# How the last squares of a norm are summed: VectorE for all eight feature tiles, and one product per token block in place of two

## The chip, the core and the metric

The kernel runs on one core of one Trainium2 chip. The core has a matrix engine (TensorE, in the profile PE, with its weight loads as PEld), a vector engine (VectorE, DVE), a scalar engine (ScalarE, ACT), a general one (GpSimd, POOL) and one that issues most transfers (SyncE, SP). Each takes its instructions in the order of its own queue and waits on semaphores for the others. The metric is the device time of one execution in microseconds (us). A change of under 0.5% is about what a measurement of this kernel cannot tell from none.

## The reference, cut to what matters

The program is one step of a two-layer model over 640 tokens of 1024 features: 512 latent tokens and 128 context tokens. Layer 0 mixes tokens by attention, layer 1 by a gated linear recurrence, and a gated feed-forward block (FFN) follows each. Ahead of each of these four sub-layers stands a normalisation, and a last one stands at the end:

```python
def _rms_norm(x, g):
    xf = x.astype(jnp.float32)
    y = xf * lax.rsqrt(jnp.mean(xf * xf, axis=-1, keepdims=True) + RMS_EPS)
    return (y * g.astype(jnp.float32)).astype(x.dtype)

def _modulate(x, g, shift, scale):
    return _rms_norm(x, g) * (1 + scale[:, None, :]) + shift[:, None, :]
```

Scale, shift and a gate for the residual come from a conditioning vector by a product with `w_mod`; latent and context tokens have their own. What the change touches is the sum of the squares over the features of a token.

## The kernel before, in words

**Layout.** Features lie on the 128 partitions, in eight tiles (`KT = 8`), tokens along the free axis. `x[:, k]` is feature tile k of the residual stream. Tokens are worked on in chunks: `CH` is 0 to 320 and 320 to 640, `CHL` is 0 to 384 and 384 to 640. A weight tile is split into a high and a low part (`unit` L163, `two` L185, `split` L1068: ScalarE casts, VectorE subtracts, L182 or L1070), and `chunk` (L209) makes a product of three matmuls for each feature tile: high by high (L217), high by low (L218), low by high (L219). Its result lies in one of a few accumulators: three with the name `mm`, and in some phases two or three named `mx`. A chunk can start only when the accumulator that it takes has been read.

**A norm.** A projection produces the new x tile by tile. For each tile and chunk `residual` (L437) adds the gated product to x on VectorE (L440) and calls `square` (L370). This squares the tile on ScalarE (L376 for tile 0, straight into the sum `ssq`; L379 into a buffer `sq`, of which there are two) and adds tiles 1 to 6 to `ssq` on VectorE (L381). The last tile, 7, isn't added: its squares are kept in `lastq`. Then `moment` (L387) sums over the partitions on TensorE: for each block of 128 tokens a single-precision product of `ssq` with a column of ones (L393), and a second one of tile 7's squares into the same place (L396). The profile records each such product as two instructions. In a chunk of 320 the third block overlaps the second. VectorE makes the variance from it (`var`, L398), GpSimd raises it to the power -1/2 (`rs`, L400), VectorE spreads that over a diagonal (`dg`, L402), and `spread` (L405) multiplies the diagonal by ones on TensorE (L410), so that each partition has the factor of each token.

**The five norms.** The first, at the start, sums all eight tiles in `ssq` by its own code (`load_x` in `start`, L316) and uses one product for each block, since `lastq` is still empty. The other four use `square`:

1. *Norm 1*, in `project` (L444) after the attention projection, ahead of the first FFN. The FFN's first matmuls use x before its normalisation; the factor is applied when their results are read (`rt`, L709 and L717). Meanwhile VectorE is filled with modulation products (L247), whose weights GpSimd loads (L243) into two buffers.
2. *Norm 2*, in `project_closing` (L458), which ends the first layer. Its chunks are those of `CHL`. The second chunk of the last six feature tiles is left to the end, and between its steps the first chunk is normalised: `normed` (L467) calls `modulate` (L413), that is L415 on VectorE, L416 on ScalarE, L417 on VectorE. Tiles 6 and 7 of this wait, by an order written by hand, behind `self.sq`, the newest addition to `ssq`. The recurrent layer's first chunk (`x0[0]` in `run`, L1183) then begins, and from feature tile 3 on it stands behind `self.at`, the last product of the sum; the next one stands behind the spread (`self.rr`), and the weight split of its unit behind `self.sq`.
3. *Norm 3*, in `project_halves` (L779) after the recurrence, ahead of the second FFN, with the chunks of `CH`. Its factor is copied by ScalarE (L799), and `first_half` (L752) normalises the first chunk (L746, L747) while the second is projected. The FFN's first products (`plain`, L891) are held behind `self.at` and `self.rr` too (`held`, L832).
4. *The final norm*, in `project_last` (L498).

**What sets the order.** Within each engine a scheduler places the instructions by its own estimate of times; orders written by hand (`issue_after`) bind it. An engine never passes a waiting instruction.

The `tail` list that is set at the start isn't used.

## Time and profile before

| | us |
|---|---|
| median of the three runs | 1538.77 |
| the three runs | 1538.27, 1538.77, 1543.96 |
| the profiled execution | 1538.44 |
| its span, first to last instruction | 1536.3 |

Of the span TensorE is busy for 97%, VectorE for 69%, ScalarE for 45%, GpSimd for 16%. The mean granted clock of TensorE was 0.989 of full speed.

The rows of the timeline that are shown below begin with the start in us from the span's start and the time in us that the row lasts, then the engine, the source line, the operation, the tile that it writes, an arrow, and the tiles that it reads, with their shapes; `x2` means two instructions merged. In brackets stand the idle time of the engine just before and what ended it. Matmuls overlap in these rows, so the pace of TensorE is read from starts, not from durations. In the list of waits the three numbers are us in total, times, and the longest. In the table of windows the columns are the window, its length, the busy us (and instructions) of PE, PEld, DVE, ACT and POOL, the granted clock, the share of the transfer engines, and GB/s.

The three norms of the change lie at about 382 to 401 us (norm 1), 839 to 870 us (norm 2) and 1058 to 1090 us (norm 3); the final one begins near 1515 us.

### The profile page before, as it was taken

Reading aid. Unit: us, or ns where it says so; the run is one execution under the profiler, and the core shown is the slowest. Engines: PE = TensorE matmul, PEld = TensorE weight load, DVE = VectorE, ACT = ScalarE, POOL = GpSimd, SP = SyncE. Lnnn points to the kernel's source line nnn. Section 1 sums busy time; section 2 is a strip of 40 time slices with the busy share of each in tenths; the row PEclk is TensorE's granted clock in tenths of the full one; section 3 lists DMA queues with packets and bytes.
Section 4 is the critical chain, followed back from the end, with each engine's and each line's share of the span. In section 5 each row is a group of like instructions: output and inputs, shape, how many; then the busy total and the mean of one; then the engine's idle time right before and its main releaser. Section 6 shows DMA issues by size and latency. Waiting matters only on the chain. (4 is left out here: it accounts for less than half of the span.)

```text
span 1536.3 us, 25993 instructions
## 1 busy us (share of the span) xinstructions
PE 1483.2 (97%) x10309; PEld 1437.0 (94%) x10309; DVE 1060.9 (69%) x2000; ACT 695.3 (45%) x1266; POOL 253.2 (16%) x270
## 2 busy tenths in 40 slices
PE   5999999989999999999999999989999999999997
PEld 3899999889999999999999988889999999999996
DVE  5668788869899987434443869874965656556556
ACT  5576667755333123312331478853544342424242
POOL 2101122100111110000000113220222322222210
PEclk9999999999999999999999999999999999999998
DMA  9545656545566664222223533334242231323211
GB/s 378 154 115 162 182 157 184 145 136 187 178 194 191 194 215 124 72 83 76 71 61 106 153 119 110 107 130 142 85 135 71 81 102 64 98 68 97 70 56 69
DMA packets 73098, 196.65 MB, mean 128 GB/s; under 512 B 8048, under 2 KB 25616, under 8 KB 72848
## 3 DMA queue, kind: packets, MB, share of 16 engines
q1 hardware_dynamic: 58832, 144.48, 29.6%
q0 software_dynamic: 13856, 50.35, 10.5%
q8 instruction: 81, 1.33, 0.4%
q14 instruction: 41, 0.34, 0.1%
q10 hardware_dynamic: 288, 0.16, 0.0%
HBM read 179.48 MB, written 8.92 MB: 123 GB/s over the span
## 5 line engine op out<-in xcount | busy, mean ns | idle before, releaser
L217 PE MATMUL mm<-big,whi 128*128 128x320 f32 (+3 forms) x1290 | 400.1, 313 | 9.0 <-ACT big L1069 7.3
L218 PE MATMUL mm<-big,whi 128*128 128x320 f32 (+3 forms) x1290 | 402.9, 313 | 2.9 <-DVE big L1070 2.2
L219 PE MATMUL mm<-big,wlo 128*128 128x320 f32 (+3 forms) x1290 | 401.9, 312 | 1.9 <-DVE wlo L182 1.6
L217 PEld LDWEIGHTS mm<-big,whi 128*128 128x128 f32 x1290 | 243.6, 190 | 13.5 <-ACT big L1069 8.2
L218 PEld LDWEIGHTS mm<-big,whi 128*128 128x128 f32 x1290 | 244.9, 190 | 6.6 <-DVE big L1070 4.3
L219 PEld LDWEIGHTS mm<-big,wlo 128*128 128x128 f32 x1290 | 244.4, 190 | 3.7 <-DVE wlo L182 2.1
L247 DVE SCALAR_TENSOR_TENSOR mprod<-mraw,csb 128x1024 f32<-128x1024 f32 x160 | 195.5, 1222 | 8.7 <-DMA mraw<-in_wm 8.4
L440 DVE SCALAR_TENSOR_TENSOR x<-mm,G,x 128x128 f32<-128x128 f32 (+3 forms) x211 | 85.5, 435 | 92.1 <-PE mm L219 91.8
L182 DVE TENSOR_TENSOR wlo<-raw,whi 128x1024 fp32r<-128x1024 f32 (+1 forms) x90 | 109.8, 1220 | 38.0 <-ACT whi L180 23.1
L180 ACT CAST whi<-raw 128x1024 fp32r<-128x1024 f32 (+1 forms) x74 | 76.8, 1037 | 121.0 <-PE mm L218 81.8
L217 PE MATMUL mm<-big,whx 128*128 128x320 f32 (+3 forms) x363 | 113.3, 312 | 0.0
L219 PE MATMUL mm<-big,wlx 128*128 128x320 f32 (+3 forms) x363 | 113.0, 311 | 0.0
L218 PE MATMUL mm<-big,whx 128*128 128x320 f32 (+3 forms) x363 | 112.7, 311 | 0.0
L243 POOL DMA_DIRECT2D mraw<-in_wm x80 | 43.3, 542 | 381.3 <-DVE mprod L247 259.1
L217 PE MATMUL mx<-big,whi 128*128 128x320 f32 (+3 forms) x278 | 86.6, 311 | 0.0
L219 PE MATMUL mx<-big,wlo 128*128 128x320 f32 (+3 forms) x278 | 86.3, 310 | 0.0
L218 PE MATMUL mx<-big,whi 128*128 128x320 f32 (+3 forms) x278 | 86.3, 310 | 0.0
L180 ACT CAST whx<-raw 128x1024 fp32r<-128x1024 f32 (+1 forms) x40 | 41.0, 1027 | 90.6 <-PE mm L218 55.1
L217 PE MATMUL mx<-big,whx 128*128 128x320 f32 (+3 forms) x245 | 75.8, 309 | 0.0
L219 PE MATMUL mx<-big,wlx 128*128 128x320 f32 (+3 forms) x245 | 75.6, 309 | 0.0
L218 PE MATMUL mx<-big,whx 128*128 128x320 f32 (+3 forms) x245 | 75.4, 308 | 0.0
L1069 ACT CAST whi<-raw 128x1024 fp32r<-128x1024 f32 (+1 forms) x41 | 41.3, 1008 | 72.8 <-PE mm L218 45.1
(295 smaller groups left out, 3602.9 us busy)
## 6 DMA issues: line engine op xcount, KB each, us to landing
raw<-in_gu SPq DMA_DIRECT2D x88, 512.0 KB, 3.6
mraw<-in_wm POOLq DMA_DIRECT2D x80, 512.0 KB, 4.1
raw<-in_dn SPq DMA_DIRECT2D x24, 512.0 KB, 3.7
raw<-in_wqk SPq DMA_DIRECT2D x16, 512.0 KB, 4.3
raw<-in_wi SPq DMA_DIRECT2D x16, 512.0 KB, 3.6
whi<-in_wi POOLq DMA_DIRECT2D x16, 512.0 KB, 4.4
raw<-in_dn SPq DMA_DIRECT2D x16, 448.0 KB, 3.4
sw<-in_wm SPq DMA_DIRECT2D x10, 512.0 KB, 10.1
```

Source lines behind the costliest of these rows:

```text
L180: nc.scalar.copy(hi, raw)
L182: nc.vector.tensor_tensor(lo, raw, hi.bitcast(F32), ALU.subtract)
L217: nc.tensor.matmul(ps, hi[:, k], xhi[:, k, s], start=(k == 0), stop=False)
L218: nc.tensor.matmul(ps, hi[:, k], xlo[:, k, s], start=False, stop=False)
L219: nc.tensor.matmul(ps, lo[:, k], xhi[:, k, s], start=False, stop=(k == nk - 1))
L243: nc.gpsimd.dma_start(w, self.i["wm"][l * 6 + j - 2, f])
L247: nc.vector.scalar_tensor_tensor(prod, w, 1.0, self.csb[:, s], ALU.mult, ALU.mult, accum_out=out[:, s, f:f + 1])
L440: self.nc.vector.scalar_tensor_tensor(xs, ps[:, a - t0:b - t0], G[:, s, f:f + 1], xs, ALU.mult, ALU.add)
L1069: self.nc.scalar.copy(hi, v)
```

## The change

In norms 1, 2 and 3 tile 7's squares are now added to `ssq` by VectorE like those of the others, and each block has one product. A flag `apart`, set in `project_last`, keeps the final norm as it was. `self.sq` is thereby the addition of tile 7 in the inner norms, and `self.at` the one product of the last block.

```diff
-        self.anchor, self.pbufs, self.lastq, self.tail = None, {}, {}, []
+        self.anchor, self.pbufs, self.lastq, self.apart = None, {}, {}, False
...
         q = self.t([P, 384], F32, "sq", 2, self.sb)[:, :t1 - t0]
         nc.scalar.activation(q, self.x[:, k, s], AF.Square)
-        if k < KT - 1:
+        if k == KT - 1 and self.apart:
+            self.lastq[t0] = q
+        else:
             self.sq = nc.vector.tensor_tensor(self.ssq[:, s], self.ssq[:, s], q, ALU.add).ins
-        self.lastq[t0] = q
...
         for j, b in enumerate(bl):
-            nc.tensor.matmul(ps[:, j:j + 1], self.ssq[:, b:b + P], self.ones[:, 0:1], start=True, stop=not self.lastq)
-            if not self.lastq:
+            self.at = nc.tensor.matmul(ps[:, j:j + 1], self.ssq[:, b:b + P], self.ones[:, 0:1], start=True, stop=not self.apart).ins
+            if not self.apart:
                 continue
             self.at = nc.tensor.matmul(ps[:, j:j + 1], self.lastq[t0][:, b - t0:b - t0 + P], self.ones[:, 0:1], start=False, stop=True).ins
...
-        first = None
+        first, self.apart = None, True
```

## The prediction, made before the changed kernel ran

> **What bounds the kernel now.** I read the page's busy line first, then what TensorE (PE) waited for, then the timeline of each engine around the three inner norms.

> ```profile
> PE 1483.2 (97%) x10309; PEld 1437.0 (94%) x10309; DVE 1060.9 (69%) x2000; ACT 695.3 (45%) x1266; POOL 253.2 (16%) x270
> ```

> ```profile
> PE mm L217 <- ACT big L1069: 7.3, 3, 6.2
> ...
> PE mx L410 <- DVE dg L402: 2.6, 2, 1.9
> ...
> PE at L393 <- DVE ssq L381: 2.0, 2, 1.7
> ```

> PE is busy for 97% of the span, and its largest wait on one cause is 7.3 us in all: what leaves PE's queue is a gain, unless a new wait takes it back. The lower two rows (total, times, longest) are waits of norms: the sum product (L393) for the sum of squares, the spread (L410) for the diagonal. The longer of each, 1.7 and 1.9, is in the final norm, which stays as it is.

> **What is removed.** A chunk of 320 or 384 tokens has three blocks of 128 (in 320 the last overlaps), one of 256 has two. The inner norms have 6 + 5 + 6 = 17 blocks, so 17 products of L396 go, each recorded as two instructions.

> ```profile
> 382.44 0.31 PE L217 MATMUL mx<-big,whi 128*128 128x320 f32 x1
> ...
> 384.07 0.31 PE L219 MATMUL mx<-big,wlo 128*128 128x320 f32 x1
> ...
> 385.03 0.36 PE L396 MATMUL at<-ones,sq 128*128 128x1 f32 x2
> 385.25 0.36 PE L393 MATMUL at<-ones,ssq 128*128 128x1 f32 x2
> ```

> Durations overlap, so I go by starts: 385.25 - 385.03 = 0.22 us for a product, (384.07 - 382.44)/11 = 0.148 us for a large matmul of 320 columns. 17 x 0.22 = **3.8 us** is the most that PE saves, or 4.0 with fewer breaks between groups. That is 0.26%, under the 0.5% that a measurement of this kernel can tell from no change.

> **What is added.** Six additions on VectorE (DVE), 0.3 to 0.5 us each, some 2.4 us in all. More matters that each sum now waits for tile 7's addition, and that the scheduler, which knows it, puts the sum products, spreads and their neighbours elsewhere. The built program differs in order only around the three norms and in how the modulation products interleave behind the first. On POOL one modulation load (L243) moves ahead of two powers (L400); on SP two stores of x each pass a neighbour. Those are read much later: I cost the stores at nothing. ScalarE's casts and squares move by a place or two, in its 55% of idle time.

> *Norm 1, after the attention projection.*

> ```profile
> 388.80 0.36 PE L396 MATMUL at<-ones,sq 128*128 128x1 f32 x2
> ...
> 398.40 0.83 PE L410 MATMUL rr<-dg,ones 128*128 128x128 f32 x6
> 398.98 0.39 PE L219 MATMUL mm<-big,wlo 128*128 128x322 f32 x1
> ...
> 401.45 0.31 PE L217 MATMUL mm<-big,whi 128*128 128x320 f32 x1
> ```

> ```profile
> 389.20 0.23 DVE L398 TENSOR_SCALAR var<-at 128x3 f32<-128x3 f32 x2 [3.15 <-PE at L396]
> 389.35 1.21 DVE L247 SCALAR_TENSOR_TENSOR mprod<-mraw,csb 128x1024 f32<-128x1024 f32 x1
> 390.49 0.08 DVE L247 DVE_READ_ACCUMULATOR mprod<-mraw,csb 128x1 f32 x1
> 391.33 0.56 DVE L402 TENSOR_TENSOR dg<-ident,rs 128x384 f32<-128x384 f32 x1 [0.76 <-POOL rs L400]
> 391.81 0.17 DVE L249 TENSOR_TENSOR G<-G,cols 128x16 f32<-128x16 f32 x1
> ```

> In before the two groups of sum products stand apart; now both stand behind 63 large matmuls counted from the one at 382.44: 382.44 + 63 x 0.148 = 391.8, six products end at 393.1, and the variance, 0.4 us after the last product's start as in before, is done at 393.4. DVE then has, in the built order, three modulation products (1.14 each) and two weight splits (as long) ahead of the second diagonal, and two diagonals of 0.48: 393.4 + 5 x 1.14 + 2 x 0.48 = 400.1, so the second spread starts at 400.2. PE is ready for it at 393.1 + 33 x 0.148 + 0.58 (first spread: 398.98 - 398.40) + 5 x 0.148 = 399.3, and waits 0.9 us. The group behind it starts at 400.2 + 0.6 = 400.8 instead of 401.45: **-0.6** of the 1.4 that PE alone would save. The additions lie in DVE's idle 3.15 us. Bounds: -1.4 (no wait); and, for the case that the products just ahead of the second diagonal find their load late, the longest such wait of the stretch behind this norm (total, times, longest):

> ```profile
> DVE mprod L247 <- DMA mraw<-in_wm: 7.9, 10, 1.8
> ```

> With 1.8 us of that and the half clock described below (1.5), -0.6 becomes +2.7.

> *Norm 2, the projection that closes the first layer.* DVE's queue sets the pace here.

> ```profile
> 846.95 0.83 PE L410 MATMUL rr<-dg,ones 128*128 128x128 f32 x6
> ```

> ```profile
> 846.42 0.60 DVE L440 SCALAR_TENSOR_TENSOR x<-mx,G,x 128x128 f32<-128x128 f32 x2
> 846.93 0.60 DVE L440 SCALAR_TENSOR_TENSOR x<-mm,G,x 128x128 f32<-128x128 f32 x2
> 847.56 0.42 DVE L381 TENSOR_TENSOR ssq<-ssq,sq 128x256 f32<-128x256 f32 x1
> 847.90 1.66 DVE L415 SCALAR_TENSOR_TENSOR nv<-x,A,rr 128x384 f32<-128x384 f32 x3
> 849.48 0.42 DVE L381 TENSOR_TENSOR ssq<-ssq,sq 128x256 f32<-128x256 f32 x1
> ...
> 856.46 0.42 DVE L381 TENSOR_TENSOR ssq<-ssq,sq 128x256 f32<-128x256 f32 x1
> 856.79 0.60 DVE L415 SCALAR_TENSOR_TENSOR nv<-x,A,rr 128x384 f32<-128x384 f32 x1
> 857.32 1.22 DVE L182 TENSOR_TENSOR wlo<-raw,whi 128x1024 fp32r<-128x1024 f32 x1
> 858.45 0.60 DVE L415 SCALAR_TENSOR_TENSOR nv<-x,A,rr 128x384 f32<-128x384 f32 x1
> 858.98 0.15 DVE L398 TENSOR_SCALAR var<-at 128x2 f32<-128x2 f32 x1
> ...
> 860.28 0.42 DVE L402 TENSOR_TENSOR dg<-ident,rs 128x256 f32<-128x256 f32 x1
> ```

> ```profile
> 856.92 0.38 PE L393 MATMUL at<-ones,ssq 128*128 128x1 f32 x2 [0.35 <-DVE ssq L381]
> ...
> 860.87 0.66 PE L410 MATMUL rr<-dg,ones 128*128 128x128 f32 x4
> 861.28 0.42 PE L217 MATMUL mm<-big,whi 128*128 128x384 f32 x1
> ```

> The first chunk's spread stands 18 matmuls of 256 columns later (0.148 x 256/320 = 0.12 each), less three products and a break: 846.95 + 2.2 - 0.8 = 848.4. The normalisation (L415) that waits for it moves from 847.90 to 849.35, and from there DVE has no gap before the sum. Up to tile 7's addition its queue holds six L415 (1.58/3 = 0.53 by starts), six L417 taken as long, six updates of x (0.51/2 = 0.26) and two additions (0.33): 8.6 us, so that addition starts at 857.9, against 856.46 for the last one now. PE gets the sum 0.46 us later, at 858.4, but is ready at 856.57 - 0.8 = 855.8: **a wait of 2.6 us where 0.35 stood**. Behind the addition stand a weight split pinned to it (1.13) and two L415, so the variance comes at 860.45, the diagonal 1.3 later as now, the second spread at 862.3, and the recurrent layer's second chunk at 862.7 instead of 861.28. That is **+1.4**, with the two removed products already in it. Queued behind are the L415 and L417 of the second chunk, 1.5 us late too. Bounds: -1.1 (PE alone), +1.4.

> *The half clock.* A wait of that length had a consequence before:

> ```profile
> 1107.60:1109.50 1.90, 0.02 (x1) 0.02 (x1) 1.90 (x4) 0.46 (x1) 0.67 (x1) 1.00 0.23 85
> 1109.50:1113.40 3.90, 3.90 (x16) 3.90 (x17) 3.90 (x11) 0.00 (x0) 0.00 (x0) 0.57 0.27 83
> 1113.40:1117.00 3.60, 3.60 (x27) 3.60 (x26) 3.60 (x7) 3.52 (x7) 2.62 (x2) 0.99 0.60 185
> ```

> After 1.9 us with PE idle (0.02 busy in the first row) the granted clock, third column from the end, was 0.57 over 3.9 us: 16 matmuls where 3.9/0.148 = 26 would fit, so ten are lost, 1.5 us. If 2.6 us do the same, the 15 matmuls of 384 columns between the sum and the spread run at 0.178/0.57 = 0.31 instead of 0.178 us: from 858.9, twelve or thirteen in the 3.9 us and the rest in 0.4 end at 863.2, and the second spread moves from 862.3 to there: **+0.9**, which I take, since the nearest row did it. Bounds: 0 and +1.5 (all of a dip exposed).

> [...]

> *Norm 3, after the recurrent layer.*

> ```profile
> 1080.54 0.68 DVE L440 SCALAR_TENSOR_TENSOR x<-mx,G,x 128x192 f32<-128x192 f32 x2 [1.30 <-PE mx L219]
> ...
> 1081.54 1.68 DVE L381 TENSOR_TENSOR ssq<-ssq,sq 128x320 f32<-128x320 f32 x3
> 1083.13 1.22 DVE L182 TENSOR_TENSOR wlo<-raw,whi 128x1024 fp32r<-128x1024 f32 x1
> ```

> ```profile
> 1088.35 0.91 PE L410 MATMUL mx<-dg,ones 128*128 128x128 f32 x6 [0.79 <-DVE dg L402]
> ```

> The second spread already waits for DVE, whose queue starts with PE's last projection chunk (the release at 1080.54). That chunk comes 0.8 us earlier (three products, one break); one addition makes the queue 0.4 longer, and some of the gaps between its additions close. I take **-0.5**; the rest of PE's saving becomes a longer wait, 1.6 for 0.79. Bounds: -1.4 and +0.4. The dip after 1107.6 I leave as it is.

> **Sum:** -0.6 + 1.4 + 0.9 - 0.5 = +1.2 us. The profiled execution took 1538.44 us around a span of 1536.3 (the median of the three runs is 1538.77): 1538.44 + 1.2 = **1539.6 us**.

> **Rivals.**
> 1. *No half clock at norm 2*: 2.6 us is short enough, or PE waits less because its queue and DVE's are closer than I count. 1538.44 + 0.3 = 1538.7. For it: PE waits for DVE up to the second spread anyway. Against: the 0.57 above. [...]
> 2. *The whole saving arrives*: the additions are in time and the moved spreads cost nothing. 1538.44 - 3.8 = 1534.6, 1534.4 with the breaks. For it: 97% busy, few waits. Against: DVE has no gap between 847.56 and the sum in norm 2.
> 3. *Slower*: PE starves at norm 1 too. The second spread there stands behind five DVE operations of 1.14 us that need loaded weights, and the next chunks have no free accumulator before it. From a wait of some 1.9 us on, the half clock sets in. With the whole queue of 5.7 us and a load 1.8 late exposed: 1538.44 - 1.4 + 5.7 + 1.8 + 1.5 + 2.3 (norm 2) - 0.5 = 1547.8. Against: in before that load lands ahead of its turn, and the moved L243 asks for it earlier still.

> That the products stay is excluded: the built program has none of the 17.

> **How the numbers follow.** Forecast 0.45, rival 1 0.25, rival 2 0.15, rival 3 0.05; the remaining 0.10 is for two starved norms or an exposed dip, about 1541 to 1543. The forecast's own range is 1538.3 to 1541.5. The range that takes in rivals 1 and 2 below and the unknown costs above (1539.6 + 0.6 + 2.7 at norm 1) is 1534.4 to 1542.9. Faster by over 0.5% needs 1530.7, which even 4.0 us cannot give: 0.01. Slower by over 0.5% is 1546.1, rival 3 alone: 0.05. Within: 0.94.

> **What would show it.** (Lines from L381 on stand one or two later in the changed kernel.) The second product left with 10 instructions, all in the final norm; the additions up from 48 to 54. At norm 2 a PE wait of 2 to 3 us for the sum and granted clock near 0.5 in the next 3 us; a second spread some 1.4 us later in step. At norm 1 a PE wait of about 0.9 for the diagonal; at norm 3 one of 1.6. It is wrong if these waits are absent and the time falls by 3 us or more, or if waits appear in the feed-forward blocks between the norms.

## The result, and the profile after

| | median, us | lowest to highest, us | executions |
|---|---|---|---|
| before | 1539.08 | 1535.31 to 1545.32 | 22 |
| after | 1544.35 | 1537.60 to 1549.09 | 22 |

The ratio is 1.0028, 95% interval 1.0017 to 1.0039: 4.3 us slower, between 2.6 and 6.0 (the two medians themselves lie 5.3 apart). That is under 0.5%, as forecast, and yet the interval tells it from none. The changed kernel is slower than the forecast says, and 1544.35 lies above the range. The profiled execution of the changed kernel took 1544.4 us around a span of 1542.5.

The page's busy line shows the work that went and the work that came:

```profile
PE 1484.9 (96%) x10275; PEld 1439.1 (93%) x10275; DVE 1065.1 (69%) x2006; ACT 694.3 (45%) x1266; POOL 254.3 (16%) x270
```

PE has 34 instructions fewer, the 17 second products; VectorE has six more, the additions (L383 now, 54 instead of 48). PE's count fell and its busy time did not: it was 1483.2. The list of waits (total, times, longest) says where to look:

```profile
PE at L394 <- DVE ssq L383: 4.1, 2, 2.4
PE mx L411 <- DVE dg L403: 3.8, 2, 2.0
```

Each of the two rows of norms has grown, from 2.0 and 2.6. The longest wait for a sum is now 2.4 us, and it is no longer in the final norm. The timeline of PE has it in norm 2, a new wait for the second diagonal at norm 1, and a longer one at norm 3 (1.95 us, before 0.79), by which the second row grew:

```profile
402.95 0.91 PE L411 MATMUL rr<-dg,ones 128*128 128x128 f32 x6 [0.58 <-DVE dg L403]
...
832.17 0.34 PE L217 MATMUL mm<-big,whx 128*128 128x384 f32 x1
...
850.61 0.83 PE L411 MATMUL rr<-dg,ones 128*128 128x128 f32 x6
...
860.50 1.01 PE L394 MATMUL at<-ones,ssq 128*128 128x1 f32 x4 [2.40 <-DVE ssq L383]
...
866.32 1.06 PE L411 MATMUL rr<-dg,ones 128*128 128x128 f32 x4
...
876.04 0.38 PE L217 MATMUL mm<-big,whi 128*128 128x256 f32 x1 [0.19 <-ACT xr L1009]
...
1093.77 0.91 PE L411 MATMUL mx<-dg,ones 128*128 128x128 f32 x6 [1.95 <-DVE dg L403]
```

Starts of two profiles can't be compared directly, since one may run late from an earlier point on. So I compare the same large matmul in both, ahead of a norm and behind it. The two rows of L217 above are these in the kernel before:

```profile
830.01 0.34 PE L217 MATMUL mm<-big,whx 128*128 128x384 f32 x1
...
870.36 0.38 PE L217 MATMUL mm<-big,whi 128*128 128x256 f32 x1 [0.37 <-ACT xr L1008]
```

The changed kernel is 832.17 - 830.01 = 2.16 us late ahead of norm 2 and 876.04 - 870.36 = 5.68 behind it: norm 2 costs **+3.52 us**. "In step" below means that the lag ahead of the norm is taken off. Counted in the same way norm 1 gives **-0.61** and norm 3 **-0.05**, together +2.86. Which matmul is taken moves such a step by up to 0.05.

The table of windows, in stretches of 3.41 us, has the rest (window, its length, PE busy, PEld, DVE, ACT, POOL, granted clock, transfer share, GB/s):

```profile
857.09:860.50 3.41, 1.01 (x6) 0.70 (x4) 3.41 (x10) 1.61 (x4) 0.00 (x0) 1.00 0.39 136
860.50:863.91 3.41, 3.41 (x12) 3.41 (x13) 3.32 (x6) 1.14 (x2) 1.06 (x1) 0.50 0.33 77
863.91:867.32 3.41, 3.41 (x14) 3.41 (x13) 1.59 (x3) 0.00 (x0) 0.29 (x7) 0.50 0.34 93
867.32:870.73 3.41, 3.41 (x21) 3.41 (x20) 3.32 (x13) 1.94 (x7) 0.00 (x0) 1.00 0.37 143
```

In the first row PE is busy for 1.01 us; in the next two it has half clock, 6.8 us in all; in the fourth the clock is whole. All 15 matmuls between the sum and the second spread run at half clock (0.32 us from start to start, against 0.17 ahead of the wait), one reason why the page's busy time of PE did not fall. VectorE, busy throughout in the first row, is busy for 1.59 us in the third: now it waits for PE, 1.84 us for the second spread.

The profiled execution is also 2.8 us late before any changed instruction. Of this 2.05 us arise between 290 and 320 us, with half clock in the attention, where this execution has it (two stretches from 300.72 on, the first is shown) and the profiled one of before has not:

```profile
297.30:300.71 3.41, 1.79 (x12) 1.16 (x10) 3.41 (x6) 3.36 (x7) 3.25 (x4) 1.00 0.42 106
300.72:304.13 3.41, 3.06 (x10) 2.66 (x11) 3.41 (x6) 3.41 (x10) 0.43 (x1) 0.50 0.00 0
```

### The profile page after: what moved, and what is told of

Same layout as the page of the kernel before. It is cut to its first block, busy times and chain, and to the rows that moved or that the text cites. A ratio compares the mean times of both kernels' runs of the same rounds, so it can differ in the third digit from the quotient of the medians.

```text
span 1542.5 us, 25932 instructions
## 1 busy us (share of the span) xinstructions
PE 1484.9 (96%) x10275; PEld 1439.1 (93%) x10275; DVE 1065.1 (69%) x2006; ACT 694.3 (45%) x1266; POOL 254.3 (16%) x270
## 5 line engine op out<-in xcount | busy, mean ns | idle before, releaser
L217 PE MATMUL mm<-big,whi 128*128 128x320 f32 (+3 forms) x1290 | 402.4, 315 | 8.9 <-ACT big L1070 7.3
L219 PE MATMUL mm<-big,wlo 128*128 128x320 f32 (+3 forms) x1290 | 404.2, 314 | 1.6 <-DVE wlo L182 1.6
L217 PEld LDWEIGHTS mm<-big,whi 128*128 128x128 f32 x1290 | 245.6, 191 | 13.3 <-ACT big L1070 8.2
L219 PEld LDWEIGHTS mm<-big,wlo 128*128 128x128 f32 x1290 | 246.4, 191 | 3.1 <-DVE wlo L182 2.1
L247 DVE SCALAR_TENSOR_TENSOR mprod<-mraw,csb 128x1024 f32<-128x1024 f32 x160 | 195.8, 1224 | 3.8 <-DMA mraw<-in_wm 3.5
L182 DVE TENSOR_TENSOR wlo<-raw,whi 128x1024 fp32r<-128x1024 f32 (+1 forms) x90 | 109.8, 1220 | 34.2 <-ACT whi L180 22.9
L217 PE MATMUL mm<-big,whx 128*128 128x320 f32 (+3 forms) x363 | 113.4, 312 | 0.0
L219 PE MATMUL mm<-big,wlx 128*128 128x320 f32 (+3 forms) x363 | 113.0, 311 | 0.0
L243 POOL DMA_DIRECT2D mraw<-in_wm x80 | 43.4, 542 | 382.6 <-DVE mprod L247 268.3
L217 PE MATMUL mx<-big,whi 128*128 128x320 f32 (+3 forms) x278 | 86.7, 312 | 0.0
L219 PE MATMUL mx<-big,wlo 128*128 128x320 f32 (+3 forms) x278 | 86.4, 311 | 0.0
L217 PE MATMUL mx<-big,whx 128*128 128x320 f32 (+3 forms) x245 | 76.0, 310 | 0.0
L219 PE MATMUL mx<-big,wlx 128*128 128x320 f32 (+3 forms) x245 | 75.6, 309 | 0.0
```

What stands on the lines that cost most here:

```text
L182: nc.vector.tensor_tensor(lo, raw, hi.bitcast(F32), ALU.subtract)
L217: nc.tensor.matmul(ps, hi[:, k], xhi[:, k, s], start=(k == 0), stop=False)
L219: nc.tensor.matmul(ps, lo[:, k], xhi[:, k, s], start=False, stop=(k == nk - 1))
L243: nc.gpsimd.dma_start(w, self.i["wm"][l * 6 + j - 2, f])
L247: nc.vector.scalar_tensor_tensor(prod, w, 1.0, self.csb[:, s], ALU.mult, ALU.mult, accum_out=out[:, s, f:f + 1])
```

## The experiments

Theory A: nearly all of the loss is made at norm 2, where VectorE's queue makes the sum late and half clock follows PE's wait. Theory B: the loss is spread over the three norms, from the added work and the moved groups. Theory C: the wait counts, half clock behind it does not reach the end. Theory D, for one run: the work that hand-written orders pin behind tile 7's addition makes the loss.

All runs against the kernel before on the same chip; the difference is the ratio of the executions times 1539.5 us, with its 95% interval. The columns of the norms are single profiled executions, in step. "Half clock" counts stretches of 3.41 us behind the sum of norm 2. Runs 9 and 10 stand below.

| run | difference, us | norm 1 | norm 2 | norm 3 | wait for the sum, us | half clock |
|---|---|---|---|---|---|---|
| the change | +4.3 [2.6, 6.0] | -0.61 | +3.52 | -0.05 | 2.40 | 2 |
| 1 norm 2 only | +1.8 [-0.3, 4.0] | 0.00 | +2.00 | -0.01 | 2.39 | 1 |
| 2 norms 1 and 3 | -2.0 [-4.2, 0.0] | -0.63 | -0.05 | -0.05 | 0.26 | 0 |
| 3 no addition | -1.7 [-4.3, 0.9] | -1.39 | 0.00 | -1.71 | 0.98 | 0 |
| 4 gap filled | -0.2 [-1.8, 1.7] | -0.63 | +1.59 | -0.05 | 0.30 | 0 |
| 5 orders at tile 6 | +6.5 [4.0, 9.1] | -0.63 | +3.13 | +2.95 | 3.53 | 1 |
| 6 four tiles behind | +0.2 [-2.0, 2.5] | -0.63 | +1.28 | -0.05 | 0.33 | 0 |
| 7 diagonal first | -2.2 [-4.2, -0.2] | -0.56 | +0.21 | -0.06 | 1.20 | 0 |
| 8 the change again | +3.4 [1.2, 5.4] | -0.61 | +3.48 | -0.05 | 2.40 | 2 |

**1 and 2: one norm alone, and the other two.** The flag is set at the head of each projection.

```diff
     def project(self, w, hi, lo, gk, nxt=None, done=None, ahead=False):
+        self.apart = True
...
     def project_closing(self, w, hi, lo, gk, key, nh, nl, xd):
+        self.apart = False
...
     def project_halves(self, w, hi, lo, gk, key, xd):
+        self.apart = True
```

This is run 1; run 2 has True in `project_closing` and False in `project_halves`.

> The addition and the single product at norm 2 only; norms 1 and 3 keep tile 7's squares apart and their second products. Theory A (nearly all of the loss is made at norm 2: PE waits about 2.4 us for the late sum and then runs on half clock): about 3.5 us over the kernel before, with a wait of 2 to 2.6 us for the sum of squares and half clock behind it. Theory B (the loss is spread over the three norms, some 1.4 us each, by the added work of VectorE and the moved groups): +1.4 us. Theory C (the wait counts, but half clock after it does not add to the end): +1.4 us, with the wait.

> The addition and the single product at norms 1 and 3; norm 2 as in the kernel before. Theory A: -0.4 us against the kernel before (norm 1 about -0.3, norm 3 about 0), no long wait at norm 2. Theory B: +2.8 us. Theory C: -0.4 us.

With norm 2 alone the wait is there, and half clock behind it; without norm 2 both are gone, and the kernel comes out at or just under the one before. PE's row in run 2:

```profile
856.57 0.38 PE L394 MATMUL at<-ones,ssq 128*128 128x1 f32 x2 [0.26 <-DVE ssq L383]
```

Theory B wanted +2.8 in run 2; the interval ends at 0.0. The loss is made at norm 2. The median of run 1 alone can't tell +3.5 from +1.4, since its interval holds both; the steps can. In run 1 there is one stretch of half clock, not two, and norm 2 costs 2.00, not 3.5:

```profile
855.92:859.33 3.41, 1.02 (x8) 0.70 (x6) 3.41 (x9) 1.36 (x3) 0.00 (x0) 1.00 0.39 137
859.33:862.74 3.41, 3.41 (x13) 3.41 (x13) 3.24 (x7) 1.14 (x2) 1.31 (x7) 0.50 0.42 118
862.74:866.15 3.41, 3.41 (x22) 3.41 (x22) 3.10 (x9) 1.30 (x5) 0.03 (x1) 1.00 0.29 76
```

```profile
859.07 0.81 PE L394 MATMUL at<-ones,ssq 128*128 128x1 f32 x4 [2.39 <-DVE ssq L383]
```

The wait and PE's 1.02 busy us are those of the changed kernel; only the row after the half-clock one differs.

**3: no addition at all.**

```diff
-        else:
+        elif k < KT - 1 or self.apart:
```

> The 17 second products are gone and nothing comes in their place: the squares of tile 7 are left out of the sums of norms 1, 2 and 3. So it shows what PE saves when no sum has to wait for the addition. Theory A: about -3 us against the kernel before (3.8 at most, less what the second spreads of norms 1 and 3 wait for their diagonal), no half clock at norm 2. Theory B, as far as the loss comes from the moved groups: between -1 and +2 us. Theory C: -3 us.

Norms 1 and 3 give 3.1 us together, at least the 12 x 0.22 = 2.6 of their products, but norm 2 gives nothing although five products are gone from it. PE's timeline says why: even tile 6's addition comes 0.98 us after PE is ready for it.

```profile
862.24 0.61 PE L394 MATMUL at<-ones,ssq 128*128 128x1 f32 x4 [0.98 <-DVE ssq L383]
```

The kernel leaves the squares of tile 7 out, so it is no candidate, only a measurement. At norm 2 VectorE sets the pace with or without the new addition, and nothing taken from PE's queue there comes back. The interval of the median, -4.3 to 0.9, is too wide to tell -3 from 0; the steps do.

**4: the gap filled.** The sum is as late as in the changed kernel, but PE works until shortly before it: twelve products, pinned behind the projection's last matmul (`lm`).

```diff
-            nc.tensor.matmul(ps, lo[:, k], xhi[:, k, s], start=False, stop=(k == nk - 1))
+            self.lm = nc.tensor.matmul(ps, lo[:, k], xhi[:, k, s], start=False, stop=(k == nk - 1)).ins
...
+        for m in range(12 if dummy else 0):
+            with self.pin(self.lm):
+                nc.tensor.matmul(ps[:, 128:512], dummy[0], dummy[1], start=True, stop=True)
         for j, b in enumerate(bl):
...
-            self.stat(t0, t1)
+            self.spread(self.moment(t0, t1, (hi[:, 0, 0:128], hi[:, 0, 0:384]) if c else None))
```

> The changed kernel with twelve extra products of 384 columns on PE (their result is read by nothing) right behind the projection of norm 2, ahead of the nine products that stand before the late sum: 2.1 us of work in a wait of 2.4. The sum comes no earlier. Theory A: no half clock at 860 to 867 us; the 15 products behind the sum take 2.7 us, not 5.8, the second spread then waits for its diagonal (done at 864.4) and starts at 864.5, not 866.3: 1.8 us below the changed kernel, about +2.5 us over the kernel before. Theory B and theory C: as the changed kernel, +4.3 us, since the sum and the diagonal are as late as there.

This run separates theory A from theory C. Its windows and its rows of PE:

```profile
855.36:858.77 3.41, 3.10 (x19) 2.79 (x17) 3.41 (x10) 1.58 (x4) 0.00 (x0) 1.00 0.44 155
858.77:862.18 3.41, 3.19 (x17) 2.60 (x17) 3.31 (x6) 1.14 (x2) 1.09 (x1) 1.00 0.34 91
```

```profile
858.74 0.61 PE L397 MATMUL at<-ones,ssq 128*128 128x1 f32 x4 [0.30 <-DVE ssq L383]
...
862.83 0.68 PE L414 MATMUL rr<-dg,ones 128*128 128x128 f32 x4
```

The profile lags by 0.40 us ahead of norm 2, so in step the sum is at 858.34. In the changed kernel it is at 860.50 - 2.16 = 858.34: equally late. But the second spread is at 862.43 in step, and not at 866.32 - 2.16 = 864.16. Norm 2 costs 1.59 instead of 3.52 us: the late sum makes **1.6**, half clock **1.9**. The median speaks against theory C too: -0.2 us with an interval that ends at 1.7, where C wanted +4.3. But the +2.5 that I had for theory A lies outside as well. I had taken 1.8 off the median of the changed kernel; the three norms of run 4 add up to +0.91, which the interval holds.

**5: the hand orders back at tile 6.**

```diff
-            self.sq = nc.vector.tensor_tensor(self.ssq[:, s], self.ssq[:, s], q, ALU.add).ins
+            add = nc.vector.tensor_tensor(self.ssq[:, s], self.ssq[:, s], q, ALU.add).ins
+            self.sq = self.sq if k == KT - 1 else add
```

> The changed kernel, but the work that is ordered by hand behind the newest addition (the weight split and the normalisation of tiles 6 and 7 at norm 2, weight splits at norm 3) stands behind tile 6's addition again, as in the kernel before. Theory A (VectorE's queue ahead of the addition makes the sum late, half clock follows the wait): the scheduler now puts the split of 1.13 us ahead of tile 7's addition, so the sum comes about 1.1 us later still, PE waits about 3.5 us for it and half clock follows; norm 2 costs 2.5 to 4.5 us, the kernel as slow as the changed one: +2 to +4.5 us over the kernel before. Theory D (the loss comes from the work pinned behind tile 7's addition): norm 2 loses under 1 us, the kernel is level with the one before or under it.

Theory D wanted norm 2 to lose under 1 us and the kernel to be level; it is slower than the changed one. The pins do not delay the sum, they protect it: without them the scheduler puts weight splits (L182) ahead of tile 7's addition, at norm 2 as I expected and at norm 3 as I had not. VectorE's rows at norm 3:

```profile
1088.97 1.22 DVE L182 TENSOR_TENSOR wlo<-raw,whi 128x1024 fp32r<-128x1024 f32 x1
1090.10 1.22 DVE L182 TENSOR_TENSOR wlx<-raw,whx 128x1024 fp32r<-128x1024 f32 x1
1091.24 1.22 DVE L182 TENSOR_TENSOR wlo<-raw,whi 128x1024 fp32r<-128x1024 f32 x1
1092.37 0.48 DVE L383 TENSOR_TENSOR ssq<-ssq,sq 128x320 f32<-128x320 f32 x1
```

PE waits 3.05 us for that addition and gets half clock there too, and norm 3 costs +2.95. What the work behind the addition costs by itself this run can't tell, since it moved ahead of it.

**6: four tiles behind the addition.**

```diff
-            with self.pin(self.sq if t0 == 0 and k > 5 else None):
+            with self.pin(self.sq if t0 == 0 and k > 3 else None):
...
-                for k in range(max(0, 2 * j - 2), 2 * j) if f < KT - 2 else ():
+                for k in range(max(0, 2 * j - 2), 2 * j) if f < KT - 3 else ():
...
-            for k in (6, 7) if c else ():
+            for k in (4, 5, 6, 7) if c else ():
```

> The changed kernel with four tiles of the first chunk's normalisation at norm 2 behind the addition, not two: two operations of L416 and two of L418, 2.1 us, leave the queue ahead of tile 7's addition, and some of them come between it and the second diagonal. Theory A: the wait for the sum falls to under 0.7 us, no half clock behind it, the second spread about 0.5 us earlier than the full-clock one of the filled kernel (862.4 in step with the kernel before), so norm 2 costs 1.0 us or a little less: +0.4 us over the kernel before in all. Theory B (added work of VectorE as such): as the changed kernel, about +4 us.

The queue ahead of the addition was the cause of its lateness: with four operations fewer there, the sum comes 2.07 us earlier in step (4 x 0.53 = 2.1), the wait for it is 0.33 us and half clock is gone. But the normalisation that was put off is now what PE waits for, one product behind the next:

```profile
853.97 0.60 PE L394 MATMUL at<-ones,ssq 128*128 128x1 f32 x4 [0.33 <-DVE ssq L383]
857.27 0.45 PE L218 MATMUL mm<-big,whi 128*128 128x384 f32 x1 [1.69 <-DVE big L418]
```

The wait has moved, and norm 2 still costs 1.28.

**7: the first diagonal ahead of a weight split.** In the changed kernel a split that waits for its load stands ahead of the first diagonal. Before, it stood behind it. The two rows of before, and those of the changed kernel:

```profile
844.11 0.56 DVE L402 TENSOR_TENSOR dg<-ident,rs 128x384 f32<-128x384 f32 x1 [1.06 <-POOL rs L400]
845.27 1.23 DVE L182 TENSOR_TENSOR wlo<-raw,whi 128x1024 fp32r<-128x1024 f32 x1 [0.61 <-DMA whi<-in_wi]
```

```profile
847.05 1.23 DVE L182 TENSOR_TENSOR wlo<-raw,whi 128x1024 fp32r<-128x1024 f32 x1 [0.49 <-DMA whi<-in_wi]
848.20 0.55 DVE L403 TENSOR_TENSOR dg<-ident,rs 128x384 f32<-128x384 f32 x1
```

In the changed kernel `rs`, which the diagonal reads, was ready at 846.44 us (on GpSimd from 845.57 on, for 0.87). VectorE was idle for 0.49 us until the split's load had landed, and the diagonal started only behind the split.

The run orders the split behind that diagonal (`dg0`):

```diff
+            self.dg0 = self.dg0 if c else self.dg
...
-            x0, g0, x1 = self.lru_xr(0, xhi, xlo), gate(0, self.sq), self.lru_xr(1, xhi, xlo, self.dg)
+            x0, g0, x1 = self.lru_xr(0, xhi, xlo, self.dg0), gate(0, self.sq), self.lru_xr(1, xhi, xlo, self.dg)
```

> The changed kernel with the first weight split of the recurrence (1.13 us, it waits for its load) ordered behind the first diagonal of norm 2, not ahead of it. The first spread then stands ten large matmuls earlier. Theory A: the chain spread, normalisation, tile 7's addition starts 1.2 us earlier; the wait for the sum is about 1.2 us, not 2.4, no half clock behind it; norm 2 costs +0.4 us and not 1.6 to 3.5: about -0.2 us against the kernel before in all. If the place of the first spread does not set the time of the sum, the wait stays at 2.4 us and the kernel stays at about +4 us.

```profile
847.50 0.83 PE L411 MATMUL rr<-dg,ones 128*128 128x128 f32 x6
...
857.39 0.60 PE L394 MATMUL at<-ones,ssq 128*128 128x1 f32 x4 [1.20 <-DVE ssq L383]
```

The wait is 1.20 us, there is no half clock, norm 2 costs +0.21. This profile is 0.24 us late ahead of norm 2, so in step the first spread comes at 847.26, 1.19 us earlier than in the changed kernel (850.61 - 2.16 = 848.45), and the sum at 857.15, also 1.19 us earlier. One instruction was ordered by hand, and most of the loss is gone: the first spread, at which VectorE's chain starts, sets the time of the sum.

**8: the changed kernel again.**

> The changed kernel as it is, a second time. Half clock has come in stretches of 3.41 us on a grid that runs through each profile; if it is set by how long PE was busy within one such stretch (under about half of it), then a wait of 2.4 us brings it when it falls into one stretch, and not when the border of two stretches cuts it in the middle. Norm 2 then costs 1.6 us without half clock, 2.0 with one stretch of it, 3.5 with two, from execution to execution; the kernel +1.0 to +2.9 us over the kernel before. If the wait itself brings it, half clock follows the wait here as well whatever the grid.

```profile
862.29 0.95 PE L394 MATMUL at<-ones,ssq 128*128 128x1 f32 x4 [2.40 <-DVE ssq L383]
```

```profile
858.97:862.38 3.41, 1.01 (x7) 0.70 (x5) 3.41 (x9) 1.52 (x4) 0.00 (x0) 1.00 0.39 135
862.38:865.79 3.41, 3.41 (x12) 3.41 (x13) 3.25 (x6) 1.14 (x2) 1.15 (x3) 0.50 0.38 98
865.79:869.20 3.41, 3.41 (x13) 3.41 (x13) 1.62 (x3) 0.00 (x0) 0.20 (x6) 0.50 0.31 83
```

Again 2.40 us of wait, 1.01 busy us of PE in the stretch and two stretches of half clock. Three profiled executions with this wait (the changed kernel, runs 1 and 8) all had half clock, so a 2.4 us wait without it, which my expectation allows for, was not seen. What was seen is the same question at another wait, in the recurrence near 925 us, where PE waits for `lt` for 1.84 to 1.91 us in every profile. Before, and the changed kernel:

```profile
922.31:925.72 3.41, 1.55 (x8) 0.87 (x8) 3.41 (x5) 2.91 (x4) 1.45 (x1) 1.00 0.22 32
925.72:929.13 3.41, 3.41 (x11) 2.37 (x10) 3.41 (x4) 2.99 (x4) 0.93 (x1) 0.50 0.41 147
```

```profile
928.77:932.18 3.41, 1.87 (x9) 1.40 (x10) 3.41 (x4) 2.65 (x4) 0.79 (x2) 1.00 0.48 143
932.18:935.59 3.41, 3.41 (x19) 2.93 (x18) 3.41 (x6) 3.38 (x5) 1.09 (x2) 1.00 0.54 124
```

The wait is the same, but the border of two stretches cuts it differently: behind 1.55 busy us came half clock, behind 1.87 not. Of the first ten profiles five have half clock there (busy 0.44 to 0.46 of the stretch) and five have not (0.46 to 0.65).

**9 and 10: a later wait filled, alone and with run 2.** Behind norm 3 PE waits 1.89 us for the halved x near 1107 us, and half clock follows in seven of the first ten profiles (not eight, as I wrote). Run 9 is the kernel before, run 10 is run 2, with twenty products pinned behind the one ahead of the wait (`m`):

```diff
-                        nc.tensor.matmul(ps, hi[:, k], xh, start=(k == 0), stop=False)
+                        m = nc.tensor.matmul(ps, hi[:, k], xh, start=(k == 0), stop=False).ins
+                    if c and n == 0 and k == KH - 1:
+                        pad = self.ps("at")[:, 0:HT]
+                        for _ in range(20):
+                            with self.pin(m):
+                                nc.tensor.matmul(pad, hi[:, k], xh, start=True, stop=True)
```

> The kernel before with twenty extra products of 320 columns (their result is read by nothing) in the wait of 1.89 us for the halved x near 1107 us, behind norm 3. It tells whether half clock behind a wait costs time elsewhere too. If it does as at norm 2: no half clock near 1110 us in the profile, 1.0 to 1.7 us less from 1105 to 1125 us in step where the kernel before has it, and about 1 us less in the median, since not every execution has it there (eight of the ten profiles so far). If half clock is hidden there: no change in step, and 0 in the median.

> The version that the runs so far point to: the addition and the single product at norms 1 and 3 only, norm 2 as in the kernel before, and the twenty products in the wait near 1107 us. By the parts: -0.7 us (norms 1 and 3 in step) and -1 us, -1.7 us against the kernel before; by the measured median of the version without the fill (-2.0 us), -3 us.

Measured: -0.3 us [-2.2, 1.5] and -0.6 us [-2.8, 1.7]; the -3 that run 2's median led me to lies outside. Half clock is gone there in both profiles, and in step next to nothing is gained (-0.14 and -0.09). But the fill was no clean one: ten products that ran ahead of the wait before now stand behind it, 10 x 0.148 = 1.5 us, about what one stretch of half clock costs. So run 9 doesn't price it. Three profiles have no half clock there without a fill, and they give a price: between 1105 and 1125 us they gain 1.57 (run 8), 1.05 (run 3) and 1.86 us (run 5) against the kernel before, with waits of 1.87, 2.38 and 1.57 us where that has 1.89. The waits taken off, all three give 1.54 or 1.55 us for one stretch among large matmuls.

A version that is clearly better than the kernel before was not found. Runs 2 and 7 beat the changed kernel; against the one before their intervals end at 0.0 and -0.2 us, in step they give -0.73 and -0.41, and run 10, which has run 2's change in it, came out at -0.6.

## Why the prediction was wrong

- **Norm 1, -0.6: right.** -0.61 in step, and -0.56 to -0.63 in the other runs with the change. The second spread waits 0.58 us for its diagonal where I had 0.9.
- **Norm 2, the late sum, +1.4: right in mechanism and size.** The first spread was to come at 848.4 and came at 848.45 in step, the sum at 858.4 and came at 858.34, the wait was to be 2.6 us and was 2.40, and without half clock (run 4) the norm costs 1.59. The cause is the one named: VectorE's queue from the first spread to tile 7's addition (runs 6 and 7).
- **Half clock, +0.9: the step that failed.** That it comes was right, and rival 1 falls with it. Its size was wrong. I took its length from one row, 3.9 us, "twelve or thirteen in the 3.9 us and the rest in 0.4", and counted these 15 matmuls alone. In both profiles of the changed kernel it lasted two stretches, 6.8 us. All 15 matmuls ran at half clock, 0.32 us from start to start, and so did what I had left out: the sum products ahead of them took 0.87 us by starts (861.37 - 860.50; 0.46 in run 4) and the second spread behind them 0.71 (867.03 - 866.32; 0.43 in run 4). That makes 1.9 us, twice my value and past my bound of 1.5. With one stretch, in run 1, it made 0.4. The row that I took was one stretch of 3.41 us with a part of its neighbours. The window that I had taken hid the border of that stretch, at 1110.04 us.
- **Norm 3, -0.5: wrong.** The last projection chunk came 0.64 us earlier in step, as expected, but behind it four additions (L383) take 1088.54 - 1086.35 = 2.19 us, where three took 1083.13 - 1081.54 = 1.59:

```profile
1085.36 0.68 DVE L441 SCALAR_TENSOR_TENSOR x<-mx,G,x 128x192 f32<-128x192 f32 x2 [1.02 <-PE mx L219]
1085.95 0.48 DVE L1071 TENSOR_TENSOR big<-x,big 128x320 fp32r<-128x320 f32 x1
1086.35 2.28 DVE L383 TENSOR_TENSOR ssq<-ssq,sq 128x320 f32<-128x320 f32 x4
1088.54 1.22 DVE L182 TENSOR_TENSOR wlo<-raw,whi 128x1024 fp32r<-128x1024 f32 x1
```

  I had 0.4 for one more addition; 0.6 took the gain, and the second spread's wait grew to 1.95 us where I had 1.6.
- **Rival 2** (the whole saving arrives) falls with run 3: even without the addition norm 2 gives nothing. **Rival 3** (norm 1 starves) falls with norm 1's -0.6; the place that starves is norm 2. Its "from a wait of some 1.9 us on" is not what the runs showed: waits of 1.84 to 1.91 us near 925 us brought half clock in some profiles and not in others, and the 1.95 us at norm 3 did not.
- **The sum.** In step it is -0.61 + 3.52 - 0.05 = +2.86 us where I had +1.2; half clock makes 1.0 of the difference, norm 3 0.45 and the late sum 0.2. On 1538.44 that would be 1541.3, on the median of before 1541.9, both inside the range. So the two sizes that I had wrong don't alone put 1544.35 above it. The rest is within the scatter of single executions, for which the range left no room: it was added up from costs of the norms on one profiled execution, which lies 0.6 us below the median of before.

  Is there a further cause beyond the three norms? The measured difference less the steps of the three norms is +1.4 us for the changed kernel and +0.6 for its repetition, but between -1.8 and +1.4 over the nine rows of the table and nothing in the mean, and each interval holds its steps. So the runs give no sign of one, though 1.4 us is too little for them to rule it out. And single executions scatter where nothing was changed. The order of instructions on PE, VectorE, ScalarE and GpSimd is the same in all twelve profiles up to 382 us, yet the large matmuls near 375 us lie between 1.67 us earlier and 6.73 later than in the profile of before. Four of them (the changed kernel, runs 3, 7 and 8) lose 2.0 to 2.15 us with half clock near 302 us; but they are spread over 4 us already at 60 us (-1.40 to +2.68), and why is open.

In the profiles of before and after half clock came in whole stretches on one grid. In the changed kernel's the granted clock goes from 1.00 to 0.50 at 27.65, 34.48, 300.72, 331.44, 860.51, 1031.17, 1116.51 and 1532.93 us, that is 2, 78, 9, 155, 50, 25 and 122 times 3.413 us apart, and up to the last, which outlasts the program, half clock is 3.41 or 6.83 us long each time. The profile of before has it from 28.02, 34.84, 328.39, 925.72, 1024.71, 1110.04 and 1526.47 us on, the starts again whole multiples of 3.413 us apart. Half clock came behind a stretch of 3.41 us in which PE was busy for 1.01 us (the changed kernel, at 860.51) and behind one with 1.55 us (before, at 925.72).

## What to carry to other kernels

When a product leaves the busiest engine, ask which engine sets the time of the instruction that now stands first: here VectorE set it, the saving stayed out, and with one more operation in its queue the wait of the matrix engine was 2.40 us where 0.35 stood. Price such a wait with what follows it, in the whole stretches in which the granted clock moved (3.41 us each here), and lay the windows on the borders of these stretches before reading a length from them. Where a wait can't be avoided, first look for one instruction at the head of the late engine's chain that can go behind it (run 7: a wait of 1.20 us, no half clock); putting work off behind the wait took half clock away here, but a wait of 1.69 us came behind it (run 6).

## What was not expected of the hardware

```profile
1106.77:1110.18 3.41, 1.61 (x11) 1.35 (x10) 3.41 (x7) 0.46 (x1) 0.93 (x1) 1.00 0.20 75
1110.18:1113.59 3.41, 3.41 (x15) 3.41 (x14) 3.41 (x10) 0.69 (x2) 0.00 (x0) 0.50 0.49 114
922.45:925.86 3.41, 1.57 (x7) 1.09 (x8) 3.41 (x4) 2.65 (x4) 0.99 (x1) 1.00 0.38 115
925.86:929.28 3.42, 3.42 (x20) 2.94 (x19) 3.42 (x5) 3.40 (x4) 1.15 (x1) 1.00 0.43 113
```

```profile
1114.97:1118.38 3.41, 1.56 (x10) 1.57 (x11) 3.41 (x8) 0.46 (x1) 0.64 (x1) 1.00 0.10 37
1118.38:1121.80 3.42, 3.42 (x26) 3.42 (x25) 3.42 (x9) 0.98 (x2) 0.09 (x1) 1.00 0.50 124
```

- That half clock makes most of the scatter of single executions, 1537.6 to 1549.1 us for the changed kernel, isn't shown. Over its 22 executions a lower mean granted clock goes with a longer time only loosely: the correlation is -0.53, a good quarter of the variance.
- The same wait of 2.4 us brought one stretch of half clock in run 1, where it ended 0.26 us before the border of two stretches (859.07 and 859.33), and two in the changed kernel, where it ended on the border (860.50) or 0.09 us before it (862.29 and 862.38, run 8). Why, no run here shows.
